# Weight tiles of two row blocks by 512 columns in the down and output projections, and up products in the order hi, hi, lo, lo

## Chip, cores and metric

The kernel runs on one core of a Trainium2 chip. The metric is the device time of one execution in microseconds (us), as the median of three runs. Beside it stands the trace of one profiled execution, whose span is counted from its first to its last instruction.

## What is computed

Two decoder layers on 256 tokens of width 2048, each an attention block and a squared-ReLU MLP, with a norm before and after each block. Cut to what matters here:

```python
D_MODEL, SEQ, D_FF = 2048, 256, 8192
def sq_relu_mlp(h, w_up, w_down):
    h = jax.nn.relu(h @ w_up)            # [256, 2048] @ [2048, 8192]
    return (h * h) @ w_down              # [256, 8192] @ [8192, 2048]

for l in range(2):
    h = rmsnorm(x, norm_attn_pre[l])
    mix = attention_l(h) @ w_o[l]        # output projection, [256, 2048] @ [2048, 2048]
    x = x + rmsnorm(mix, norm_attn_post[l])
    h = rmsnorm(x, norm_mlp_pre[l])
    x = x + rmsnorm(sq_relu_mlp(h, w_up[l], w_down[l]), norm_mlp_post[l])
```

Everything is float32. The weights amount to about 348 MB, each read once.

## The kernel before

[...] In the text below one "product" is one matmul instruction with its weight load. The 256 tokens are two halves of 128 (hf 0 and hf 1).

Weights come in tiles of 512 KB through `weights` (L115): SyncE issues the DMA into one of three `raw` buffers, ScalarE writes `hi`, VectorE writes `lo`, each into one of six buffers. TensorE takes them in the order of the program.

There are two ways of multiplying. With the activations stationary (`mm_tok`, L199, whose three products are L200, L201 and L202) the moving operand is 512 columns of weights, and a bank of PSUM holds [128 tokens, 512 columns]. `head_proj` (K and V, and the first 512 up features of an MLP) and `col_pass` (output projection and down projection) do so. With the weights stationary, `up_feat` (L496) makes the other up features: a bank per 128 features, where the hi part of a weight block meets x's hi and lo parts side by side (512 columns, L506), and the lo part meets x's hi part alone (256 columns, L507). `q_proj` (L268, L270, L271) does the same with three products of 256 columns.

`col_pass` (L390) covers 2048 rows by 1024 columns of a weight matrix with four banks, two column chunks c by two token halves. Its tile is one row block (128 rows) by 1024 columns; a tile serves 12 products, and the bank changes after every three. The last `ahead` tiles go to half 0 first; then half 0's two banks are taken away by `evac`, `between` follows, half 1 gets the same tiles, and its two banks are taken away. `head_proj` has tiles of two row blocks by 512 columns, and there six products in a row go to one bank:

```python
for j in range(2):
    k = 2 * i + j
    mm_tok(acc[hf], *halves(xT, k, hf), hl[0][:, j], hl[1][:, j], k == 0, k == KT - 1)
```

An output projection is two passes (`o_proj`, L420), both on the four banks of tag "a", with `ahead` 1 and 5; its `evac` is a square sum on ScalarE and a multiplication by the gain on VectorE (`ug`, L429). A down projection is four times two passes (`mlp`), on tag "b" and then "a", with `ahead` 1 but for the layer's last, which has 5; its `evac` adds to an accumulator on VectorE (`mlp`, L460). After a layer's last pass `add_normed` (L168) makes the new x, half by half, and its transposes (L184) begin the next projection, or the result is stored.

A tile scheduler sets the order of instructions on each engine from the order of the code and its own estimates.

Of the kernel before, what the change touches and what calls it, by code (L numbers as in the profile page):

```python
"""Two decoder layers (sliding-window attention with sinks, then MoBA attention on a shared K/V),
each followed by a squared-ReLU MLP, on one core.

Float32 products: TensorE multiplies 12-bit significands in one pass, so every operand is split
exactly into hi + lo (float32r, 12 bits each), and a product is hi*hi + hi*lo + lo*hi, accumulated in
float32; what is left out lies below float32's own rounding.

With SEQ == MOBA_BLOCK there is one MoBA block: no block lies fully in the past, so the top-k part
is masked for every token by the shapes alone, and the own block is causal attention.
"""  # L10
# [17 lines left out]
P = 128  # L28
T = 256
NH = 2  # L30
D = 2048
KT = D // P
# [7 lines left out]
EPS = 1e-6  # L40
# chunks by which token half 0 runs ahead where it does; buffers of raw and of split weights
# [3 lines left out]
# rounds of the running projection after which a group's attention steps go: scores, transposes, mixes  # L45
# [10 lines left out]
def trunk(ctx: ExitStack, tc: tile.TileContext, x, w_qkv_a, sinks_a, w_o_a, kv_norm, w_kv_shared,  # L56
# [8 lines left out]
    # one table set serves every activation used here  # L65
    nc.scalar.preload_act_table_set("natural_log_exp_and_others")

    # ---- residual stream, by token half
# [9 lines left out]
    # ---- constants  # L78
    ident = pool.tile([P, P], F32, name="ident")
    make_identity(nc, ident)  # L80
    # the array's clock rises with use: work on nothing until x is there
# [6 lines left out]
    # gains that act on the contraction axis, as columns [p, kt]  # L88
# [13 lines left out]
    # minus the distance between query and key, for the second query block against both key blocks;  # L102
    # the last 128 columns are also the first block's
# [11 lines left out]
    # ---- weights, split on the way in  # L115
    def weights(src, shape, gain=None):
        """src: DRAM view [128, a, b] with a * b = 1024 -> its hi and lo parts. With a gain (index, k-tile),
        row block i is scaled by the gain's k-tile + i first."""
        raw = pool.tile([P, *shape], F32, tag="raw", bufs=RBUFS, name="raw")
        hi = pool.tile([P, *shape], F32R, tag="hi", bufs=WBUFS, name="hi")  # L120
        lo = pool.tile([P, *shape], F32R, tag="lo", bufs=WBUFS, name="lo")
        nc.sync.dma_start(raw, src)
        if gain is None:
            nc.scalar.activation(hi, raw, AF.Copy)  # L124
            nc.vector.tensor_sub(lo, raw, hi.bitcast(F32))  # L125
        else:
            for i in range(shape[0]):
                c = gain[0] * KT + gain[1] + i
                g = gcol[:, c:c + 1]
                nc.scalar.activation(hi[:, i], raw[:, i], AF.Copy, scale=g)  # L130
                nc.vector.scalar_tensor_tensor(lo[:, i], raw[:, i], g, hi[:, i].bitcast(F32),  # L131
                                               op0=ALU.mult, op1=ALU.subtract)
        return hi, lo
# [4 lines left out]
    # ---- norms  # L138
    def rstd_of(parts):
        """1 / sqrt(sum(parts) / D + EPS), by exp(-ln / 2) and a Newton step."""  # L140
# [19 lines left out]
    def x_rstd(hf):  # L160
        a = parts_tile()
        # x's transposes are awaited, its scale is not yet
        with tc.issue_after(turned[0]):
            for c in range(4):
                square_sum(a[:, c:c + 1], xs[hf][:, c * 512:(c + 1) * 512])
        return rstd_of(a)

    def add_normed(hf, ug, parts, each):  # L168
        """x += rstd(parts) * ug, by columns of 512; each(c) follows."""
# [6 lines left out]
    def to_T(dst, name):  # L176
        """x's 512 columns c of a token half, transposed into dst: [d, kt, (hi: both halves | lo: both halves)]."""
# [20 lines left out]
    # ---- products with the activations stationary: out [tok, n]  # L198
# [5 lines left out]
    def head_proj(xT, w, c0, gi, second=None):  # L204
        """x @ 512 columns of w from c0, by token half; half 0 starts ahead. second() makes half 1's xT."""
# [22 lines left out]
    def kv_evac(acc, r):  # L228
        """k as [d; d] rows by group (hi | lo) and v as (hi | lo) columns by group."""
# [24 lines left out]
    # ---- products with the weights stationary: out [n, tok]  # L254
    def q_proj(xT, w, g, gi):
        """The eight heads of group g, [d, tok] / 8, as rows [hi; lo] (even heads) or [lo; hi] (odd); the
        tokens' rstd is left to the scores."""
        acc = [bank("a", f"q{i}") for i in range(2)]
        for i in range(KT // 2):
            hi, lo = weights(rows(w, 2 * i, 2, g * 512, 512), (2, 512), (gi, 2 * i))  # L260
            for j in range(2):
                k = 2 * i + j
                t = xT[k // 4][:, k % 4]
                for f in range(4):
                    o = acc[f // 2][:, (f % 2) * T:(f % 2 + 1) * T]
                    fs = slice(f * P, (f + 1) * P)
                    # the first product into the bank clears it; the bank's other half then starts from clear
# [19 lines left out]
    # ---- attention, in steps that run between the rounds of a projection  # L287
# [5 lines left out]
    def rounds(n):  # L293
        """n rounds of a projection have been issued: issue the steps that are due."""
# [7 lines left out]
    def attention(g, qs, ks, vs, oT, dist, with_sink, r, std):  # L302
        def scores(qb, hp):
# [6 lines left out]
            for e in range(2):  # L310
# [4 lines left out]
                # score = (q k + bias std) rstd  # L315
# [43 lines left out]
        def mix(qb, b):  # L359
# [6 lines left out]
            # rows 0-63 came of v's hi part, rows 64-127 of its lo part; odd heads go to the upper rows  # L366
# [23 lines left out]
    def col_pass(xT, w, r0, p, tag, ahead, evac, between=None):  # L390
        """x @ w[r0:r0 + 2048, p * 1024:...] by token half: the last `ahead` row blocks go to half 0 first.
        evac(hf, c, bank) takes the sums away; between() follows half 0's."""
        ps = [[bank(tag, f"o{hf}{c}") for c in range(2)] for hf in range(NH)]

        def step(hf, k, hl):
            for c in range(2):
                cs = slice(c * 512, (c + 1) * 512)
                mm_tok(ps[hf][c], *halves(xT, k, hf), hl[0][:, cs], hl[1][:, cs], k == 0, k == KT - 1)

        tail = []  # L400
        for k in range(KT):
            r = r0 + k * P
            hl = weights(w[r:r + P, p * 1024:(p + 1) * 1024], (1024,))
            step(0, k, hl)
            rounds(1)
            if k < KT - ahead:
                step(1, k, hl)
                rounds(1)
            else:
                tail.append((k, hl))  # L410
        for c in range(2):
            evac(0, 2 * p + c, ps[0][c])
        if between:
            between()
        for k, hl in tail:
            step(1, k, hl)
        for c in range(2):
            evac(1, 2 * p + c, ps[1][c])

    def o_proj(oT, w, gain, each):  # L420
        """x += rmsnorm(o @ w) * gain."""
# [9 lines left out]
        col_pass(oT, w, 0, 0, "a", 1, evac)  # L431
# [3 lines left out]
    # ---- MLP  # L435
    def mlp(xT, wu, wd, gi, gain, r_of, each):
        """x += rmsnorm(relu(rmsnorm(x) @ wu)^2 @ wd) * gain."""
# [33 lines left out]
    def over_partitions(r):  # L471
        """The two columns r, as rows side by side on every partition."""
# [9 lines left out]
    def up_tok(acc, r, hT):  # L482
        """relu(r acc)^2 of 512 features [tok, f], transposed."""
# [12 lines left out]
    def up_feat(xT, w, c0, gi, rb, hT, tag):  # L496
        """The same with the weights stationary: x's hi and lo parts side by side, summed on the way out."""
        acc = [bank(tag, f"u{f}") for f in range(4)]
        for i in range(KT // 2):
            hi, lo = weights(rows(w, 2 * i, 2, c0, 512), (2, 512), (gi, 2 * i))  # L500
            for f in range(4):
                fs = slice(f * P, (f + 1) * P)
                for j in range(2):
                    k = 2 * i + j
                    t = xT[k // 4][:, k % 4]
                    nc.tensor.matmul(acc[f], hi[:, j, fs], t, start=(k == 0), stop=False, skip_group_check=True)  # L506
                    nc.tensor.matmul(acc[f][:, :T], lo[:, j, fs], t[:, :T], start=False, stop=(k == KT - 1),  # L507
                                     skip_group_check=True)
        for f in range(4):
# [21 lines left out]
    # ---- two layers  # L531
# [54 lines left out]
```

## Time and profile before

| | |
|---|---|
| Median of three runs | 1967.25 us (1966.46 to 1967.7) |
| Profiled execution | span 1962.4 us; its own time is not given apart from the runs |
| Median less span | 4.85 us, start and end of the execution |
| TensorE busy | 1934.3 us, 99% of the span, 10318 products |
| TensorE weight loads busy | 1653.1 us, beside the products |
| VectorE / ScalarE / GpSimd busy | 1276.7 / 1096.5 / 245.4 us |
| DMA | 354.22 MB, mean 181 GB/s |
| Granted TensorE clock, mean | 0.998 of full speed |

Products overlap in their records: one of 512 columns is recorded as about 0.39 us long, and the next starts some 0.23 us after it. So the busy share doesn't tell how fast products follow each other. The distance from start to start does, and the timeline shows it. A name such as `o<-hi,h` is output, then moving and stationary operand.

### The profile page before, as it was taken

What the parts mean: (1) busy time and instruction counts of PE and PEld (TensorE: products, weight loads), DVE (VectorE), ACT (ScalarE), POOL (GpSimd) and SP (SyncE); (2) the same over time, 40 slices, a digit from 0 to 9 for tenths busy, and PEclk for the clock granted to TensorE, in tenths of its full rate; (3) what the DMA queues carried; (4) which work ended last, traced back from release to release, by engine and by line L of the source; (5) the groups of instructions that cost most, each with busy time, mean ns of one, the idle gap of its engine ahead of it and who ended that gap; (6) DMA issues with size and microseconds to landing.
All of it is one profiled execution on the core that took longest, in us unless ns stands there. A gap on an engine that the chain in (4) does not pass through costs nothing.

```text
span 1962.4 us, 28154 instructions
## 1 busy us (share of the span) xinstructions
PE 1934.3 (99%) x10318; PEld 1653.1 (84%) x10318; DVE 1276.7 (65%) x2177; ACT 1096.5 (56%) x1977; POOL 245.4 (13%) x306
## 2 busy tenths in 40 slices
PE   8999999999999999999999999999999999999997
PEld 7998788888888888888889988888888888888886
DVE  6898577546655664675588884875466457556654
ACT  7787565445544553554477874754455345435542
POOL 0242001000100110010112420010011001100111
PEclk9999999999999999999999999999999999999999
DMA  7534656666666666666554446566666666666663
GB/s 227 161 109 149 196 163 212 196 192 191 185 191 194 183 188 191 181 189 195 168 165 150 128 148 194 166 201 198 189 183 192 199 189 183 193 192 188 187 189 123
DMA packets 140682, 354.22 MB, mean 181 GB/s; under 512 B 10912, under 2 KB 11008, under 8 KB 140032
## 3 DMA queue, kind: packets, MB, share of 16 engines
q1 hardware_dynamic: 139776, 348.17, 58.4%
q10 hardware_dynamic: 736, 4.24, 0.6%
q8 instruction: 81, 1.33, 0.3%
q14 instruction: 57, 0.47, 0.1%
q0 software_dynamic: 32, 0.02, 0.0%
HBM read 350.28 MB, written 2.10 MB: 180 GB/s over the span
## 4 chain that ended last, share of the span: by engine, by line
PE 86%; DVE 5%; ACT 5%; DMA 2%; issue 1%; DVEq 0%; POOL 0%; ACTq 0%; SPq 0%
PE u L506 23%; PE o L202 14%; PE o L201 14%; PE o L200 14%; PE u L507 12%; ACT pr L338 1%; PE q L271 1%; PE q L268 1%; PE q L270 1%; ACT hi L130 1%; PE kv L200 1%; DVE pr L325 1%; PE kv L201 1%; PE kv L202 1%; DVE lo L131 1%
## 5 line engine op out<-in xcount | busy, mean ns | idle before, releaser
L506 PE MATMUL u<-xm,hi 128*128 128x512 f32 x1920 | 676.1, 397 | 0.0
L131 DVE SCALAR_TENSOR_TENSOR lo<-raw,gcol,hi 128x512 fp32r<-128x512 f32 x672 | 487.6, 756 | 192.8 <-ACT hi L130 181.8
L125 DVE TENSOR_TENSOR lo<-raw,hi 128x1024 fp32r<-128x1024 f32 x320 | 396.5, 1239 | 328.4 <-ACT hi L124 323.9
L130 ACT ACTIVATE hi<-raw,gcol 128x512 fp32r<-128x512 f32 x672 | 455.4, 716 | 257.6 <-PE u L506 114.8
L124 ACT ACTIVATE hi<-raw 128x1024 fp32r<-128x1024 f32 x320 | 338.6, 1059 | 404.4 <-PE o L202 320.4
L507 PE MATMUL u<-xm,lo 128*128 128x256 f32 x1920 | 539.3, 281 | 0.0
L506 PEld LDWEIGHTS u<-xm,hi 128*128 128x128 f32 x1920 | 360.4, 188 | 87.2
L202 PE MATMUL o<-hi,h 128*128 128x512 f32 x1024 | 401.7, 392 | 0.0
L201 PE MATMUL o<-lo,h 128*128 128x512 f32 x1024 | 401.4, 392 | 0.0
L200 PE MATMUL o<-hi,h 128*128 128x512 f32 x1024 | 399.1, 390 | 0.0
L507 PEld LDWEIGHTS u<-xm,lo 128*128 128x128 f32 x1920 | 362.9, 189 | 0.3
L514 POOL TENSOR_TENSOR us<-us,rb 128x256 f32<-128x256 f32 x120 | 115.8, 965 | 1268.1 <-DVE us L513 1268.1
L200 PEld LDWEIGHTS o<-hi,h 128*128 128x128 f32 x1024 | 192.3, 188 | 42.9
L201 PEld LDWEIGHTS o<-lo,h 128*128 128x128 f32 x1024 | 192.3, 188 | 42.7
L202 PEld LDWEIGHTS o<-hi,h 128*128 128x128 f32 x1024 | 192.4, 188 | 40.3
L268 PE MATMUL q<-xa,hi 128*128 128x256 f32 x512 | 147.1, 287 | 0.0
L271 PE MATMUL q<-xa,lo 128*128 128x256 f32 x512 | 144.8, 283 | 0.0
L270 PE MATMUL q<-xa,hi 128*128 128x256 f32 x512 | 144.4, 282 | 0.0
L516 ACT ACTIVATE h<-uh 128x256 fp32r<-128x256 f32 x120 | 50.2, 418 | 101.1 <-DVE uh L515 101.1
L200 PE MATMUL o<-hi,o 128*128 128x512 f32 x256 | 101.5, 398 | 2.1 <-DVE ug L429 2.0
L202 PE MATMUL o<-hi,o 128*128 128x512 f32 x256 | 101.1, 395 | 0.4 <-POOL o L378 0.4
L515 DVE SCALAR_TENSOR_TENSOR uh<-us 128x256 f32<-128x256 f32 x120 | 50.8, 423 | 77.5 <-POOL us L514 77.5
(116 smaller groups left out, 1902.6 us busy)
## 6 DMA issues: line engine op xcount, KB each, us to landing
raw<-in_w_up_dram SPq DMA_DIRECT2D x256, 512.0 KB, 4.2
raw<-in_w_down_dram SPq DMA_DIRECT2D x256, 512.0 KB, 4.5
raw<-in_w_qkv_a_dram SPq DMA_DIRECT2D x40, 512.0 KB, 4.4
raw<-in_w_o_a_dram SPq DMA_DIRECT2D x32, 512.0 KB, 4.5
raw<-in_w_q_b_dram SPq DMA_DIRECT2D x32, 512.0 KB, 3.9
raw<-in_w_o_b_dram SPq DMA_DIRECT2D x32, 512.0 KB, 3.8
raw<-in_w_kv_shared_dram SPq DMA_DIRECT2D x8, 512.0 KB, 4.0
x<-in_x_dram SPq DMA_DIRECT2D x8, 256.0 KB, 5.2
```

The lines of the kernel that those rows point to most:

```text
L124: nc.scalar.activation(hi, raw, AF.Copy)
L125: nc.vector.tensor_sub(lo, raw, hi.bitcast(F32))
L130: nc.scalar.activation(hi[:, i], raw[:, i], AF.Copy, scale=g)
L131: nc.vector.scalar_tensor_tensor(lo[:, i], raw[:, i], g, hi[:, i].bitcast(F32), op0=ALU.mult, op1=ALU.subtract)
L200: nc.tensor.matmul(ps, xh, wh, start=first, stop=False)
L201: nc.tensor.matmul(ps, xh, wl, start=False, stop=False)
L202: nc.tensor.matmul(ps, xl, wh, start=False, stop=last)
L268: nc.tensor.matmul(o, hi[:, j, fs], t[:, :T], start=(k == 0 and f % 2 == 0), stop=False, skip_group_check=True)
L270: nc.tensor.matmul(o, hi[:, j, fs], t[:, T:], start=False, stop=False, skip_group_check=True)
L271: nc.tensor.matmul(o, lo[:, j, fs], t[:, :T], start=False, stop=(k == KT - 1), skip_group_check=True)
L506: nc.tensor.matmul(acc[f], hi[:, j, fs], t, start=(k == 0), stop=False, skip_group_check=True)
L507: nc.tensor.matmul(acc[f][:, :T], lo[:, j, fs], t[:, :T], start=False, stop=(k == KT - 1), skip_group_check=True)
```

## The change

`col_pass` takes tiles of two row blocks by 512 columns instead of one by 1024, so six products in a row go to a bank. A tile of column chunk c is used by both halves, then the chunk changes; at the end of a pass the last row blocks of chunk 0 come before those of chunk 1 (`late`). `evac` follows a bank's last product at once. The first pass of the output projection has `ahead` 2 instead of 1. In `up_feat` the two row blocks' hi products of a feature chunk come first, then the two lo products.

```diff
     def col_pass(xT, w, r0, p, tag, ahead, evac, between=None):
         ps = [[bank(tag, f"o{hf}{c}") for c in range(2)] for hf in range(NH)]
-        def step(hf, k, hl):
-            for c in range(2):
-                cs = slice(c * 512, (c + 1) * 512)
-                mm_tok(ps[hf][c], *halves(xT, k, hf), hl[0][:, cs], hl[1][:, cs], k == 0, k == KT - 1)
+        n = KT // 2
+        def step(hf, i, c, hl):
+            for j in range(2):
+                k = 2 * i + j
+                mm_tok(ps[hf][c], *halves(xT, k, hf), hl[0][:, j], hl[1][:, j], k == 0, k == KT - 1)
+            if i == n - 1:
+                evac(hf, 2 * p + c, ps[hf][c])
+        late = (ahead + 1) // 2
+        tiles = [(i, c) for i in range(n - late) for c in range(2)]
+        tiles += [(i, c) for c in range(2) for i in range(n - late, n)]
         tail = []
-        for k in range(KT):
-            r = r0 + k * P
-            hl = weights(w[r:r + P, p * 1024:(p + 1) * 1024], (1024,))
-            step(0, k, hl)
+        for t, (i, c) in enumerate(tiles):
+            hl = weights(rows(w, r0 // P + 2 * i, 2, p * 1024 + c * 512, 512), (2, 512))
+            step(0, i, c, hl)
             rounds(1)
-            if k < KT - ahead:
-                step(1, k, hl)
+            if t < len(tiles) - ahead:
+                step(1, i, c, hl)
                 rounds(1)
             else:
-                tail.append((k, hl))
-        for c in range(2):
-            evac(0, 2 * p + c, ps[0][c])
+                tail.append((i, c, hl))
         if between:
             between()
-        for k, hl in tail:
-            step(1, k, hl)
-        for c in range(2):
-            evac(1, 2 * p + c, ps[1][c])
+        for i, c, hl in tail:
+            step(1, i, c, hl)
...
-        col_pass(oT, w, 0, 0, "a", 1, evac)
+        col_pass(oT, w, 0, 0, "a", 2, evac)
...
             for f in range(4):
                 fs = slice(f * P, (f + 1) * P)
                 for j in range(2):
                     k = 2 * i + j
-                    t = xT[k // 4][:, k % 4]
-                    nc.tensor.matmul(acc[f], hi[:, j, fs], t, start=(k == 0), stop=False, skip_group_check=True)
-                    nc.tensor.matmul(acc[f][:, :T], lo[:, j, fs], t[:, :T], start=False, stop=(k == KT - 1),
+                    nc.tensor.matmul(acc[f], hi[:, j, fs], xT[k // 4][:, k % 4], start=(k == 0), stop=False,
                                      skip_group_check=True)
+                for j in range(2):
+                    k = 2 * i + j
+                    nc.tensor.matmul(acc[f][:, :T], lo[:, j, fs], xT[k // 4][:, k % 4, :T], start=False,
+                                     stop=(k == KT - 1), skip_group_check=True)
```

The first place is TensorE at the start of the first down pass of layer 0, before the change. `o00` is the bank of half 0 and chunk 0, `o11` that of half 1 and chunk 1; the moving operand is a part of a weight tile, the stationary one a part of the MLP's hidden activations `h00`.

```order
L200 MATMUL o00_4090<-hi_4095,h00_3177 128x512
L201 MATMUL o00_4090<-lo_4096,h00_3177 128x512
L202 MATMUL o00_4090<-hi_4095,h00_3177 128x512
L200 MATMUL o01_4091<-hi_4095,h00_3177 128x512
L201 MATMUL o01_4091<-lo_4096,h00_3177 128x512
L202 MATMUL o01_4091<-hi_4095,h00_3177 128x512
L200 MATMUL o10_4092<-hi_4095,h00_3177 128x512
L201 MATMUL o10_4092<-lo_4096,h00_3177 128x512
L202 MATMUL o10_4092<-hi_4095,h00_3177 128x512
```

The bank changes after every three products. The same place on TensorE after the change:

```order
L200 MATMUL o00_4090<-hi_4095,h00_3177 128x512
L201 MATMUL o00_4090<-lo_4096,h00_3177 128x512
L202 MATMUL o00_4090<-hi_4095,h00_3177 128x512
L200 MATMUL o00_4090<-hi_4095,h00_3177 128x512
L201 MATMUL o00_4090<-lo_4096,h00_3177 128x512
L202 MATMUL o00_4090<-hi_4095,h00_3177 128x512
L200 MATMUL o10_4092<-hi_4095,h00_3177 128x512
L201 MATMUL o10_4092<-lo_4096,h00_3177 128x512
L202 MATMUL o10_4092<-hi_4095,h00_3177 128x512
```

Six products (two row blocks) now go to `o00` before the other half's bank `o10` follows with the same tile.

The second place is TensorE in `up_feat`, before the change; `u0` to `u3` are the banks of four feature chunks, `xm00` a part of x, `hi` and `lo` a weight tile.

```order
L506 MATMUL u0_4686<-xm00_3060,hi_4715 128x512
L507 MATMUL u0_4686<-xm00_3060,lo_4716 128x256
L506 MATMUL u0_4686<-xm00_3060,hi_4715 128x512
L507 MATMUL u0_4686<-xm00_3060,lo_4716 128x256
L506 MATMUL u1_4687<-xm00_3060,hi_4715 128x512
```

The 512-column and the 256-column products take turns. The same place on TensorE after the change (x2 is two such instructions in a row):

```order
L508 MATMUL u0_4686<-xm00_3060,hi_4715 128x512 x2
L512 MATMUL u0_4686<-xm00_3060,lo_4716 128x256 x2
L508 MATMUL u1_4687<-xm00_3060,hi_4715 128x512 x2
L512 MATMUL u1_4687<-xm00_3060,lo_4716 128x256 x2
L508 MATMUL u2_4688<-xm00_3060,hi_4715 128x512 x2
```

Two of 512 columns are followed by two of 256, still four products per bank.

The third place is VectorE where the two passes of layer 0's output projection meet, before the change; `lo_...<-raw` is a split of a weight tile, `ug` the multiplication that frees a bank.

```order
L125 TENSOR_TENSOR lo_2843<-raw_2841,hi_2842 128x1024
L125 TENSOR_TENSOR lo_2861<-raw_2859,hi_2860 128x1024
L429 TENSOR_TENSOR ug0_2186<-o00_2190,grow_2184 128x512
L429 TENSOR_TENSOR ug0_2186<-o01_2191,grow_2184 128x512
L429 TENSOR_TENSOR ug1_2187<-o10_2192,grow_2184 128x512
L429 TENSOR_TENSOR ug1_2187<-o11_2193,grow_2184 128x512
```

After the change, where the same multiplications are on L432:

```order
L125 TENSOR_TENSOR lo_2843<-raw_2841,hi_2842 128x1024
L432 TENSOR_TENSOR ug0_2186<-o00_2190,grow_2184 128x512
L432 TENSOR_TENSOR ug0_2186<-o01_2191,grow_2184 128x512
L432 TENSOR_TENSOR ug1_2187<-o10_2192,grow_2184 128x512
L125 TENSOR_TENSOR lo_2861<-raw_2859,hi_2860 128x1024
L432 TENSOR_TENSOR ug1_2187<-o11_2193,grow_2184 128x512
```

The multiplications stand one split earlier, and a split lies between the third and the fourth.

## Rows read from the trace of the kernel before

**Rows 1.** The page: span, and busy time of each engine (x instructions).

```profile
span 1962.4 us, 28154 instructions
PE 1934.3 (99%) x10318; PEld 1653.1 (84%) x10318; DVE 1276.7 (65%) x2177; ACT 1096.5 (56%) x1977; POOL 245.4 (13%) x306
```

**Rows 2.** The page: the chain that ended last, share of the span by engine.

```profile
PE 86%; DVE 5%; ACT 5%; DMA 2%; issue 1%; DVEq 0%; POOL 0%; ACTq 0%; SPq 0%
```

**Rows 3.** Groups of TensorE instructions by line: shape, count, busy us, mean ns, idle before.

```profile
L506 PE MATMUL u<-xm,hi 128*128 128x512 f32 x1920 | 676.1, 397 | 0.0
L507 PE MATMUL u<-xm,lo 128*128 128x256 f32 x1920 | 539.3, 281 | 0.0
L202 PE MATMUL o<-hi,h 128*128 128x512 f32 x1024 | 401.7, 392 | 0.0
...
L202 PE MATMUL o<-hi,o 128*128 128x512 f32 x256 | 101.1, 395 | 0.4 <-POOL o L378 0.4
```

**Rows 4.** Windows: length, busy PE, PEld, DVE, ACT, POOL (x), PEclk, DMA share, GB/s.

```profile
292.20:357.50 65.30, 65.30 (x380) 57.59 (x379) 45.50 (x73) 38.54 (x65) 8.41 (x8) 1.00 0.67 206
...
445.50:535.90 90.40, 90.40 (x513) 78.44 (x512) 58.64 (x96) 50.00 (x86) 12.65 (x12) 1.00 0.64 186
535.90:623.70 87.80, 87.80 (x386) 72.07 (x385) 46.51 (x53) 37.80 (x44) 2.96 (x4) 1.00 0.64 192
...
1264.00:1330.70 66.70, 66.70 (x381) 57.86 (x380) 46.32 (x75) 38.41 (x65) 7.99 (x8) 1.00 0.67 204
...
1418.60:1507.40 88.80, 88.80 (x513) 78.25 (x513) 57.98 (x95) 49.92 (x86) 12.62 (x12) 1.00 0.63 185
```

**Rows 5.** Timeline of TensorE, second down pair of layer 0: start, length.

```profile
535.93 0.39 PE L200 MATMUL o<-hi,h 128*128 128x512 f32 x1
...
623.82 0.40 PE L506 MATMUL u<-xm,hi 128*128 128x512 f32 x1
```

**Rows 6.** Timeline of TensorE, `head_proj` of layer 0.

```profile
28.02 0.39 PE L200 MATMUL kv<-hi,xa 128*128 128x512 f32 x1
...
34.82 0.39 PE L200 MATMUL kv<-hi,xa 128*128 128x512 f32 x1
```

**Rows 7.** Timeline of TensorE, a stretch of layer 0's output projection.

```profile
179.31 0.40 PE L200 MATMUL o<-hi,o 128*128 128x512 f32 x1
...
184.21 0.40 PE L200 MATMUL o<-hi,o 128*128 128x512 f32 x1
```

**Rows 8.** Timeline of TensorE, `q_proj` of layer 0.

```profile
43.24 0.28 PE L268 MATMUL q<-xa,hi 128*128 128x256 f32 x1
...
44.68 0.28 PE L268 MATMUL q<-xa,hi 128*128 128x256 f32 x1
```

**Rows 9.** What TensorE waited for: us in total, times, longest.

```profile
PE o L200 <- DVE ug L429: 2.0, 2, 1.6
...
PE pt L184 <- DVE x L173: 1.2, 2, 0.8
```

**Rows 10.** Timeline, between the passes of layer 0's output projection.

```profile
217.16 0.39 PE L202 MATMUL o<-hi,o 128*128 128x512 f32 x1
...
218.37 2.48 DVE L429 TENSOR_TENSOR ug<-o,grow 128x512 f32<-128x512 f32 x4
...
219.11 0.50 PE L200 MATMUL o<-hi,o 128*128 128x512 f32 x1 [1.57 <-DVE ug L429]
```

**Rows 11.** Timeline of the end: last product, last sums, their norm.

```profile
1951.77 0.40 PE L202 MATMUL o<-hi,h 128*128 128x512 f32 x1
1951.89 1.28 DVE L460 TENSOR_TENSOR mlp<-o,mlp 128x512 f32<-128x512 f32 x2
1953.98 0.16 DVE L142 TENSOR_REDUCE stat<-parts 128x1 f32<-128x4 f32 x1 [0.80 <-ACT junk L153]
```

**Rows 12.** DMA issues: count, KB each, us from issue to landing.

```profile
raw<-in_w_up_dram SPq DMA_DIRECT2D x256, 512.0 KB, 4.2
raw<-in_w_down_dram SPq DMA_DIRECT2D x256, 512.0 KB, 4.5
```

## Prediction

> **What bounds the kernel now.** First the page: TensorE is busy for 1934.3 us of a span of 1962.4 us, 99%, and no other engine for more than 65% of it [rows 1]. The chain that ended last says the same: 86% of it is TensorE, 5% each VectorE and ScalarE [rows 2]. So an edit counts if it changes how fast products follow each other on TensorE, or one of the few waits between them.
>
> The busy share can't tell the first, since products overlap: 512 columns are recorded as 392 to 397 ns [rows 3], while 384 of them fit into 87.89 us [rows 5]. So I read distances from start to start. The reader is to see four things.
>
> - A down pass pair makes 384 products of 512 columns from 535.93 to 623.82 us: 228.9 ns each, 686.7 ns for three [rows 5]. The other down pairs read alike.
> - `head_proj`, same shapes, goes through 30 products in 6.80 us, 226.7 ns each, 680.0 ns for three [rows 6]. All four runs of it settle there within a few products, and no stretch of `col_pass` does.
> - A stretch of the output projection takes 4.90 us for 21 products, 233.3 ns each, 700.0 for three [rows 7].
> - The up stretches between down pairs have two lengths for the same 512 products: 90.4 us and 88.8 us, that is 353.1 and 346.9 ns for a pair of 512 and 256 columns. The first stretch of layer 0 has the short pace too (65.3 us for its 377 products), that of layer 1 the long one (66.7 us). So 7 of the 30 calls of `up_feat` go fast and 23 slowly [rows 4].
>
> The granted clock is 1.00 in all of these windows [rows 4], the level of 2.4 GHz. There 512 columns last 213.3 ns, so a product costs 13.4, 15.6 or 20.0 ns beyond its columns, and this remainder differs between places with equal shapes. In none of these stretches does TensorE wait.
>
> **The change part by part.**
>
> *Six products per bank.* The down and output projections have 1024 + 256 groups of three products [rows 3]; their number, shapes and weight loads stay. What changes is that a bank gets six products of two row blocks, from a tile of two row blocks by 512 columns. That is what `head_proj` does, in its part where the token halves take turns, and rows 6 are from this part. No row shows it inside `col_pass`, so I bound it: at best 680.0 ns for three, the pace of [rows 6], 6.7 ns less than now, 1280 × 6.7 = 8.5 us gained; at worst 700.0 ns [rows 7], 13.3 ns more, 17.1 us lost. I take the first, since the order of banks, moving tiles and stationary parts is then that of `head_proj`. What stays different is where the stationary operand lies: activations of the MLP or of attention, not x. That is what I am unsure of.
>
> *Hi, hi, lo, lo.* The 1920 pairs now cost 448 × 346.9 + 1472 × 353.1 ns = 675.2 us. The new order makes 960 groups of four: two of 512 columns, two of 256. Products of 256 columns in a row stand in `q_proj`: 12 in 1.44 us, 120.0 ns each [rows 8], so a weight load is covered by 256 columns there. For the two of 512 columns I have 226.7 to 233.3 ns [rows 6, 7]. The group costs 693.4 ns at best, 706.6 ns at worst. I take 228.9 ns, the pace of the longest run of them [rows 5]: 2 × 228.9 + 2 × 120.0 = 697.8 ns, 669.9 us in all, a gain of 5.3 us. The ends are a gain of 9.5 and a loss of 3.1 us.
>
> *The meeting of the two passes of the output projection.* Both use the same four banks. Now all four sums of half 0 and half 1 come free in a bunch: the last product of the first pass starts at 217.16 us, VectorE begins the four multiplications at 218.37, and TensorE starts the second pass at 219.11 [rows 10]. In both layers together this wait is 2.0 us [rows 9]. With the change a bank is taken away as soon as its last product is through, and from there to the first product of the new pass in the same bank 18 others follow (4.1 us), for each of the four. The split put between the third and fourth multiplication (1.2 us on VectorE) fits into that. I take the whole 2.0 us; the bounds are 0 and 2.0.
>
> *The end.* After the last product VectorE adds two chunks in 1.28 us before the norm starts [rows 11]. Chunk 0's sum of half 1 will be ready three tiles earlier and be taken away beside products, so half of it goes, 0.6 us; the norm and the store behind it stay.
>
> *The layer's ends in between.* Half 0's chunk 0 is likewise taken away three tiles earlier, so its norm starts up to 0.6 us sooner; TensorE now waits 1.2 us for x there, in two places [rows 9]. But VectorE works through splits of coming weights between the steps of that norm, which decide as much. I take 0.7 us, within 0 and 1.2.
>
> *The transfers.* Same bytes and count per tile, in runs of 2 KB instead of 4 KB. The up tiles have such runs already: they land 4.2 us after issue, the down tiles 4.5 us [rows 12], and a down tile lasts 12 × 228.9 ns = 2.7 us with three in flight. The DMA share is 0.63 to 0.65 in either kind of stretch [rows 4]. I count nothing. What hides it is that lead: ScalarE is busy 37.8 us of a pair's 87.8 [rows 4], so it catches up after a late tile. Without this cover each late tile would stop TensorE by what it is late.
>
> *Sum.* 8.5 + 5.3 + 2.0 + 0.6 + 0.7 = 17.1 us. From the profiled execution: 1962.4 − 17.1 = 1945.3 us of span, and 4.85 us around it, the distance of that span to the median of the runs, makes 1950 us.
>
> **The rivals.**
>
> *Neither pace moves.* The remainder per product is something that the order of products doesn't touch; then only the waits go, 3.3 us, 1964 us. For it: the two paces of `up_feat` come out of one and the same order, and so don't follow from the order alone [rows 4]. Against it: `head_proj` and `col_pass` have equal shapes and keep apart every time [rows 5, 6]. [...]
>
> *One pace moves, the other doesn't.* The projections reach 680.0 ns and the up products stay: 8.5 + 3.3 us, 1955 us. Or the up products gain and the projections stay at 686.7: 5.3 + 3.3, 1959 us. For it: the two edits share no product.
>
> *The projections fall into the slow pace.* The place is `col_pass` in all down passes: 700.0 ns for three, as in [rows 7], where the same code runs at that pace for 21 products without a wait. With the other terms kept that is 17.1 − 5.3 − 3.3 = 8.5 us more, 1976 us. It decides from 696.5 ns for three on: there the loss, 9.8 × 1280 = 12.5 us, has eaten the other 8.6 us and 3.9 us (0.2%) besides. Against it: it occurs only in the output projections, among attention's products.
>
> **How the numbers follow.** Both paces move as in the sum: 0.45, 1950 us. One of them: 0.22, 1955 to 1959 us. Neither: 0.15, 1964 us. Slow pace: 0.15, 1976 us. The remaining 0.03 is for what I don't see. The range reaches from 1943 us (the sum with 9.5 for the up products and 1.2 for the layers' ends is 1945; 2 us for finer errors) to 1970 us (neither pace, with the up products' 3.1 us loss, is 1967; the same margin and a little). It leaves out the slow pace and the rest. 0.2% is 3.9 us, about what a measurement of this kernel can tell from no change. Faster by more: both, one, and a small part of neither, 0.71. Within it: most of neither, 0.13. Slower: 0.16.
>
> **What would show it.** In the changed kernel's timeline: three products of a down pass in 680 ns, a down pair of 384 in 87.0 us instead of 87.9; four up products in about 698 ns, a stretch of 512 in 89.3 us, alike in all layers; no wait of L200 for `ug`; a norm that begins 0.6 us sooner after the last product. The prediction is wrong if the down pairs still take 87.9 us or 89.6 us (700 ns for three), if products of 512 columns in a row are slower in `up_feat` than anywhere before, or if TensorE begins to wait for `hi` or `lo` in the down passes.

## The result, and the profile after

In all that follows, every operand stands as the sum of two parts, hi and lo, and the product of two operands is made as three matmuls: hi hi, hi lo and lo hi.

| | before | after |
|---|---|---|
| Median | 1966.86 us (4 runs, 1966.29 to 1967.7) | 1956.03 us (4 runs, 1955.51 to 1957.04) |
| Ratio | | 0.9945, 95% interval 0.9933 to 0.9957 |
| Span of the profiled execution | 1962.4 us | 1954.3 us |

The time fell by 10.8 us, 0.55%. Span and median differ by 4.5 us before and by 1.7 us after, so the two spans alone make the gain look smaller, 8.1 us. The table before the change calls its 4.85 us the start and end of the execution, and that is wrong: in every run whose span is on record the time exceeds the span by 1.7 to 2.1 us. The rest is that the profiled execution of before was a short one. One reason shows: from 14 to 18 us its granted clock was 1.00, the level of 2.4 GHz, where the profile after has a mean of 0.81 and a second profile of before (run 11 below, span 1965.0 us) one of 0.55, so that both spent part of that time at 1.2 GHz. The forecast is not touched by this, since it adds the same 4.85 us back.

The page of the changed kernel, span and busy time, beside [rows 1]:

```profile
span 1954.3 us, 28151 instructions
PE 1928.2 (99%) x10318; PEld 1649.4 (84%) x10318; DVE 1273.6 (65%) x2177; ACT 1097.2 (56%) x1977; POOL 247.1 (13%) x306
```

TensorE is the bound as before, with the same number of products. Its windows, two up stretches of layer 0, a down pair, and two up stretches of layer 1 (columns as in [rows 4]):

```profile
291.35:357.16 65.81, 65.81 (x381) 57.46 (x380) 46.43 (x75) 38.61 (x66) 8.41 (x8) 1.00 0.71 210
445.07:534.25 89.18, 89.18 (x513) 77.81 (x512) 58.58 (x97) 49.84 (x86) 12.66 (x12) 1.00 0.65 188
534.25:622.16 87.91, 87.91 (x386) 72.13 (x385) 47.90 (x55) 37.78 (x44) 2.95 (x4) 1.00 0.64 190
1259.50:1325.30 65.80, 65.80 (x381) 57.45 (x379) 46.47 (x75) 38.80 (x67) 8.14 (x8) 1.00 0.68 206
1413.20:1502.40 89.20, 89.20 (x514) 77.83 (x513) 58.59 (x97) 49.81 (x86) 12.53 (x12) 1.00 0.65 189
```

The reader is to see two things. An up stretch of 512 products takes 89.2 us in either layer, where [rows 4] had 90.4 and 88.8: 696.7 ns for two pairs. The down pair takes 87.91 us for its 384 products, as in [rows 5]: 228.9 ns each, 687 for three. Six products per bank changed nothing there.

What TensorE waits for, the longest waits, beside [rows 9]:

```profile
PE po L364 <- ACT ph L355: 2.4, 4, 1.0
PE kv L200 <- ACT xa L187: 2.1, 1, 2.1
PE po L365 <- DVE pl L356: 1.7, 5, 0.6
PE pt L184 <- DVE x L173: 1.7, 2, 1.5
```

The wait for `ug` is gone from the whole list. The waits of the transposes (L184) for x have grown, from 1.2 to 1.7 us, the longest from 0.8 to 1.5. Another wait of the kernel before, in the K and V projection of layer 1, is gone instead:

```profile
PE kv L201 <- DVE stat L145: 0.7, 1, 0.7
```

The place of the wait for `ug` in the timeline after the change, beside [rows 10]:

```profile
217.63 1.89 DVE L432 TENSOR_TENSOR ug<-o,grow 128x512 f32<-128x512 f32 x3
...
218.08 0.39 PE L202 MATMUL o<-hi,o 128*128 128x512 f32 x1
...
218.37 0.50 PE L200 MATMUL o<-hi,o 128*128 128x512 f32 x1
```

The second pass starts 0.29 us after the last product of the first, where there were 1.95 us. At the end of the kernel, beside [rows 11], VectorE has one chunk left to add:

```profile
1944.23 0.40 PE L202 MATMUL o<-hi,h 128*128 128x512 f32 x1
1944.67 0.69 DVE L463 TENSOR_TENSOR mlp<-o,mlp 128x512 f32<-128x512 f32 x1 [0.19 <-PE o L202]
1946.15 0.16 DVE L142 TENSOR_REDUCE stat<-parts 128x1 f32<-128x4 f32 x1 [0.79 <-ACT junk L153]
```

Where the gain came from, in us, by stretches from one stage's first product to the next's in the two timelines:

| stretch | before | after | difference |
|---|---|---|---|
| eight up stretches | 678.1 | 671.5 | -6.5 |
| output projections (two) | 209.8 | 207.9 | -1.9 |
| K and V projection of layer 1, and the down pair ahead of it | 117.6 | 116.6 | -1.0 |
| last down pair to the end | 98.3 | 97.7 | -0.6 |
| the other six down pairs | 527.4 | 527.4 | 0.0 |

These make -10.0 us. The rest, +1.9 us in this pair of traces, lies in the start and in the attention stretches, which the change doesn't touch and which differ by as much between the two profiles of the kernel before: 1.4 us in the K and V projection of layer 0 and 1.1 us in the attention stretch of layer 1.

### The profile page after: what moved, and what is told of

It is laid out like the page before. It is cut to its first block, busy times and chain, and to the rows that moved or that the text cites. A ratio compares the mean times of both kernels' runs of the same rounds, so it can differ in the third digit from the quotient of the medians.

```text
span 1954.3 us, 28151 instructions
## 1 busy us (share of the span) xinstructions
PE 1928.2 (99%) x10318; PEld 1649.4 (84%) x10318; DVE 1273.6 (65%) x2177; ACT 1097.2 (56%) x1977; POOL 247.1 (13%) x306
## 4 chain that ended last, share of the span: by engine, by line
PE 87%; DVE 5%; ACT 5%; DMA 2%; issue 1%; POOL 0%; DVEq 0%; ACTq 0%; SPq 0%
PE u L508 23%; PE o L200 15%; PE o L202 15%; PE o L201 14%; PE u L512 11%; ACT pr L338 1%; DVE lo L131 1%; DVE pr L325 1%; ACT hi L130 1%; PE kv L200 1%; PE kv L201 1%; PE kv L202 1%; PE q L271 1%; PE q L268 1%; PE q L270 1%
## 5 line engine op out<-in xcount | busy, mean ns | idle before, releaser
L508 PE MATMUL u<-xm,hi 128*128 128x512 f32 x1920 | 603.5, 395 | 0.0
L512 PE MATMUL u<-xm,lo 128*128 128x256 f32 x1920 | 377.9, 278 | 0.0
L508 PEld LDWEIGHTS u<-xm,hi 128*128 128x128 f32 x1920 | 293.0, 189 | 0.7
```

The source lines that it names most:

```text
L508: nc.tensor.matmul(acc[f], hi[:, j, fs], xT[k // 4][:, k % 4], start=(k == 0), stop=False, skip_group_check=True)
L512: nc.tensor.matmul(acc[f][:, :T], lo[:, j, fs], xT[k // 4][:, k % 4, :T], start=False, stop=(k == KT - 1), skip_group_check=True)
```

## Experiments

The open question was why the down and output projections kept their 687 ns for three products. **Theory S**, later made precise as **theory R**: the pace is set by where the stationary operand lies in memory beside the moving one. In the built programs each tile has a fixed byte offset within a partition; weights and x begin at 96 modulo 128, the projections' stationary operands (attention output, hidden activations) at 32, and the change alters none of these. **Rival H**: a stretch takes over its pace from what ran before it and keeps it. Two more runs share the gain out among the parts of the change.

**1. The up order alone.** The kernel before, with this part of the change:

```diff
                 for j in range(2):
                     k = 2 * i + j
-                    t = xT[k // 4][:, k % 4]
-                    nc.tensor.matmul(acc[f], hi[:, j, fs], t, start=(k == 0), stop=False, skip_group_check=True)
-                    nc.tensor.matmul(acc[f][:, :T], lo[:, j, fs], t[:, :T], start=False, stop=(k == KT - 1),
+                    nc.tensor.matmul(acc[f], hi[:, j, fs], xT[k // 4][:, k % 4], start=(k == 0), stop=False,
                                      skip_group_check=True)
+                for j in range(2):
+                    k = 2 * i + j
+                    nc.tensor.matmul(acc[f][:, :T], lo[:, j, fs], xT[k // 4][:, k % 4, :T], start=False,
+                                     stop=(k == KT - 1), skip_group_check=True)
```

> The kernel before with the up order hi, hi, lo, lo alone. Theory A (the up order is what pays, through the pace of up_feat): the up stretches of 512 products take 89.2 us each, in every layer, as in the changed kernel, instead of 90.4 or 88.8; the time falls by 6 to 8 us, to about 1959.5. Rival B (the waits at the ends of passes carry the gain, and the up stretches' paces differ from execution to execution anyway): under 2 us, 1965 or more.

Measured: 1960.13 us (5 runs, 1959.98 to 1962.21) beside 1966.69 us of before on the same chip, ratio 0.9968 (0.9956 to 0.9981), 6.6 us less. One up stretch and the down pair after it:

```profile
445.70:534.86 89.16, 89.16 (x513) 77.80 (x512) 58.48 (x96) 49.95 (x87) 12.67 (x12) 1.00 0.64 189
534.86:622.77 87.91, 87.91 (x386) 72.12 (x385) 46.60 (x53) 37.77 (x44) 2.96 (x4) 1.00 0.64 193
```

All six full up stretches take 89.2 us. Theory A holds: the order pays by the pace.

**2. The projections' part alone.** The changed kernel with the old up order:

```diff
                 for j in range(2):
                     k = 2 * i + j
-                    nc.tensor.matmul(acc[f], hi[:, j, fs], xT[k // 4][:, k % 4], start=(k == 0), stop=False,
+                    t = xT[k // 4][:, k % 4]
+                    nc.tensor.matmul(acc[f], hi[:, j, fs], t, start=(k == 0), stop=False, skip_group_check=True)
+                    nc.tensor.matmul(acc[f][:, :T], lo[:, j, fs], t[:, :T], start=False, stop=(k == KT - 1),
                                      skip_group_check=True)
-                for j in range(2):
-                    k = 2 * i + j
-                    nc.tensor.matmul(acc[f][:, :T], lo[:, j, fs], xT[k // 4][:, k % 4, :T], start=False,
-                                     stop=(k == KT - 1), skip_group_check=True)
```

> The changed kernel with the old up order, so the new tiles, the earlier sums and ahead 2 alone. Theory A: only waits go, 2.0 us where the output projection's passes meet and 0.6 us at the end; 1964 us, down stretches of 384 products still 87.9 us, up stretches at 90.4 or 88.8. Rival B: most of the gain is here, 1958 to 1960.

Measured: 1962.22 us (11 runs, 1961.41 to 1965.54), ratio 0.9979 (0.997 to 0.9988), 4.5 us less. Down pairs take 87.9 us, up stretches 88.8 or 90.4:

```profile
447.20:535.95 88.75, 88.75 (x514) 78.25 (x513) 58.53 (x97) 49.72 (x85) 12.63 (x12) 1.00 0.65 187
535.95:623.84 87.89, 87.89 (x386) 72.11 (x385) 47.92 (x56) 37.78 (x44) 2.97 (x4) 1.00 0.64 193
623.84:714.28 90.44, 90.44 (x513) 78.39 (x512) 59.51 (x98) 49.32 (x84) 12.62 (x12) 1.00 0.64 188
```

So no pace moved, and what went is waits: 4.5 us where theory A said 2.6. A left out the K and V projection of layer 1, which is 0.8 us shorter in this trace. The two parts, 6.6 and 4.5, make 11.1 us beside the 10.8 measured for both together, well within the intervals.

**3. The changed kernel with 64 unused bytes** per partition, so that the projections' stationary operands begin at 96 modulo 128, like the weights:

```diff
+        pad = pool.tile([P, 16], F32, tag="pad", bufs=1, name="pad")
+        nc.gpsimd.memset(pad, 0.0)
         ks = pool.tile([P, HKV, 2, T], F32R, tag="k", bufs=1, name="ks")
```

> The changed kernel with 64 bytes per partition of unused memory put ahead of the tiles of k, so that the stationary operands of the projections begin at the same place modulo 128 bytes as weights and x do (they are 64 bytes off in both kernels). Theory S (the projections' pace is set by where the stationary operand lies beside the moving one, not by the order): three products go from 687 to 680 ns as in head_proj, 1280 x 6.7 = 8.6 us less, 1947.5. Rival H (the pace is taken over from what ran before, up_feat, and kept): no change, 1956, 687 ns.

Measured: 1948.01 us (4 runs, 1947.9 to 1949.73), ratio 0.9907 (0.9892 to 0.9922). An up stretch and the down pair behind it:

```profile
444.87:534.03 89.16, 89.16 (x513) 77.80 (x512) 58.61 (x97) 49.84 (x86) 12.66 (x12) 1.00 0.65 189
534.03:621.08 87.05, 87.05 (x386) 72.07 (x385) 47.83 (x55) 37.80 (x44) 2.97 (x4) 1.00 0.65 191
```

The down pair goes from 87.91 to 87.05 us, 680 ns for three, with every instruction in the same order as in the changed kernel but for the fill of the unused bytes. What runs ahead of it is the same up stretch. H falls, S holds, in its size too: 8.0 us of the 8.6 expected.

**4. The kernel before with the same 64 bytes.** The same two lines, put into the kernel before.

> The kernel before with the same 64 bytes. Theory S alone: three products per bank reach 680 ns too, 8.6 us less, 1958. If place and six products per bank are both needed: 687 ns, 1967, while the changed kernel with the 64 bytes reaches 680. Rival H: 687 ns in both, 1967.

Measured: 1962.06 us (11 runs, 1957.78 to 1965.34), ratio 0.9974 (0.9965 to 0.9983), 4.6 us less. The windows:

```profile
449.50:539.94 90.44, 90.44 (x513) 78.47 (x512) 58.61 (x96) 50.00 (x86) 12.60 (x12) 1.00 0.64 186
539.94:627.01 87.07, 87.07 (x387) 72.08 (x385) 46.58 (x53) 37.77 (x44) 2.98 (x4) 1.00 0.64 195
```

With three products per bank the down pairs reach 680 ns for three as well. The place alone does it: at both places tried with both orders of banks, the order has no part in the pace. The time gave back only half of the 8.6 us. In this profile seven of the eight up stretches have the long pace (before: six), 1.7 us, and the output projection of layer 0 takes 2.0 us longer. Most of the latter is clock. TensorE waited 1.9 us for `ug` where the two passes meet, and then the granted clock fell, to a mean of 0.75 and 0.83 in two windows of 4 us:

```profile
221.00:225.00 4.00, 3.54 (x11) 2.87 (x12) 3.32 (x5) 1.67 (x5) 0.00 (x0) 0.75 0.69 232
225.00:229.00 4.00, 4.00 (x16) 3.18 (x15) 1.22 (x1) 1.20 (x2) 0.00 (x0) 0.83 0.51 137
```

In between, eight products follow each other at 0.43 us instead of 0.23, the level of 1.2 GHz, which costs 1.6 us. Whether that is so in the other ten runs no profile tells; two of them, 1957.78 and 1958.38 us, are where theory S put the time.

**5. Everything at 0 modulo 128.** Run 3's lines, and unused bytes ahead of x's tiles:

```diff
+    pad0 = pool.tile([P, 8], F32, name="pad0")
+    nc.gpsimd.memset(pad0, 0.0)
     xT = []
     turn_x = to_T(xT, "xa0")
```

> The changed kernel with 32 unused bytes per partition ahead of x's transposed tiles and 64 ahead of k, so that all operands of products begin at a multiple of 128 bytes. Theory R (what counts is the place of the stationary operand relative to the moving one, modulo 128): as with the 64 bytes alone, 680 ns for three products, 1948. Theory L (the remaining 13 ns per product come from beginning off a multiple of 64, so full alignment takes more away): three products under 675 ns, the up stretches under 88 us, 1930 or less.

Measured: 1948.35 us (4 runs, 1945.98 to 1949.58), ratio 0.9894 (0.9877 to 0.991). Down pair 87.06 us, up stretch 89.17 us, as in run 3. L falls: starting at a multiple of 128 bytes takes nothing off the 680 ns.

**6. x at 32.** Three pads: ahead of x's tiles, behind them, and run 3's ahead of k:

```diff
+    pad0 = pool.tile([P, 16], F32, name="pad0")
+    nc.gpsimd.memset(pad0, 0.0)
     xT = []
     turn_x = to_T(xT, "xa0")
     for c in range(4):
         turn_x(0, c)
+    pad1 = pool.tile([P, 16], F32, name="pad1")
+    nc.gpsimd.memset(pad1, 0.0)
```

> The changed kernel with x's transposed tiles at 32 modulo 128, weights and the projections' stationary operands at 96. Theory R (relative place): head_proj, whose stationary operand is x, goes from 680 to 687 ns for three; the projections at 680; up_feat and q_proj, where x is the moving operand, change their pace too. Theory P (the stationary operand's own place, 32 being slow): head_proj 687, projections 680, up_feat and q_proj as in the changed kernel. Rival H (pace taken over from what ran before): head_proj stays at 680.

Measured, one run: 1946.12 us. `head_proj` goes at 687 ns for three, the projections at 680, and up stretches take 88.76 us: all three kinds moved. (Run 12 has the lines of the same kernel.) The projections and `head_proj` have changed roles against the changed kernel, with the same code. Against run 3 only x's tiles have moved modulo 128, and only the products that read x have changed their pace. R holds, P has its first two marks but not the third.

**7. The projections' stationary operand at 0, weights at 96**, by a longer pad ahead of k alone:

```diff
+        pad = pool.tile([P, 24], F32, tag="pad", bufs=1, name="pad")
+        nc.gpsimd.memset(pad, 0.0)
         ks = pool.tile([P, HKV, 2, T], F32R, tag="k", bufs=1, name="ks")
```

> The changed kernel with the projections' stationary operands at 0 modulo 128, weights at 96, a distance of 32 bytes where the changed kernel has 64. Theory R: neither 680 nor necessarily 687 ns for three; if the distance modulo 64 counts, up to 700. Theory P: 680, if only 32 is a bad place.

Measured, one run: 1973.62 us, 17.6 more than the changed kernel's median, but on a chip where the kernel before took 2.4 us more than in the result. In the traces the down pairs are 13.4 us longer than the changed kernel's and the output projections 1.6, 15.0 together. The down pair:

```profile
539.18:628.78 89.60, 89.60 (x387) 72.15 (x385) 47.96 (x55) 37.80 (x44) 2.96 (x4) 1.00 0.62 187
```

700 ns for three, the pace of [rows 7] and of the third rival of the prediction, now from start to end of every down pass. P falls.

**8. Everything at 32.** As run 5, with a longer pad ahead of x's tiles:

```diff
-    pad0 = pool.tile([P, 8], F32, name="pad0")
+    pad0 = pool.tile([P, 16], F32, name="pad0")
```

> The changed kernel with all operands of products at 32 modulo 128. Theory R: distance 0 everywhere, so 680 ns for three in head_proj and in the projections, about 1948. Theory P: 687 ns in both, about 1957.

Measured, one run: 1948.57 us; down pair 87.07 us, up stretch 89.16 us. R: distance 0, wherever the operands lie.

**9. x and the projections' stationary operands at 64.** As run 6, with other pads:

```diff
-    pad0 = pool.tile([P, 16], F32, name="pad0")
+    pad0 = pool.tile([P, 24], F32, name="pad0")
...
-    pad1 = pool.tile([P, 16], F32, name="pad1")
+    pad1 = pool.tile([P, 8], F32, name="pad1")
...
-        pad = pool.tile([P, 16], F32, tag="pad", bufs=1, name="pad")
+        pad = pool.tile([P, 8], F32, tag="pad", bufs=1, name="pad")
```

> The changed kernel with x's transposed tiles and the projections' stationary operands at 64 modulo 128, weights at 96. Stationary less moving is then 96 in head_proj and in the projections, 32 in up_feat and q_proj, two distances not seen there yet. Theory R, if the pace depends on the distance alone: head_proj and the projections agree with each other, whatever it is; 700 ns for three if 96 is as 32 (a symmetric rule), 680 or less if the order counts. Rival: head_proj and the projections differ, so something else in them counts too.

Measured, one run: 1979.61 us. An up stretch and a down pair, then two products of `head_proj` that lie ten groups of three apart:

```profile
451.23:541.17 89.94, 89.94 (x513) 78.41 (x512) 58.66 (x97) 49.90 (x86) 12.62 (x12) 1.00 0.64 185
541.17:630.77 89.60, 89.60 (x386) 71.98 (x385) 47.97 (x55) 37.77 (x44) 2.96 (x4) 1.00 0.64 189
```

```profile
27.77 0.39 PE L200 MATMUL kv<-hi,xa 128*128 128x512 f32 x1
...
34.77 0.39 PE L200 MATMUL kv<-hi,xa 128*128 128x512 f32 x1
```

700 ns for three in both, so they agree, and 96 is as 32.

**10. x at 0.** As run 6, with other pads:

```diff
-    pad0 = pool.tile([P, 16], F32, name="pad0")
+    pad0 = pool.tile([P, 8], F32, name="pad0")
...
-    pad1 = pool.tile([P, 16], F32, name="pad1")
+    pad1 = pool.tile([P, 24], F32, name="pad1")
```

> The changed kernel with x's transposed tiles at 0, weights and the projections' stationary operands at 96. Stationary less moving is 32 in head_proj, 0 in the projections, 96 in up_feat and q_proj. Theory R: head_proj 700 ns for three as the projections were at 32, projections 680; up_feat at some new pace, alike in all eight stretches.

Measured, one run: 1955.43 us. `head_proj` at 700 ns for three (7.00 us for ten groups), projections at 680, the six full up stretches at 90.02 us and the two shorter ones at 68.61, alike in both layers. As R says.

**11. The kernel before, profiled again**, with no edit.

> The kernel before, unchanged, profiled once more. If the two paces of up_feat (88.8 and 90.4 us for 512 products) are picked anew in each execution: other stretches go fast than in the first profile. If they are fixed by the program: stretch 1 of layer 0 and stretch 2 of layer 1 are fast again, the others slow.

Measured: 1967.13 us, span 1965.0. The first up stretch of layer 0 in the first profile, then the same one and the next two in this one:

```profile
289.67:357.60 67.93, 67.92 (x396) 59.63 (x395) 48.13 (x79) 40.29 (x68) 8.41 (x8) 1.00 0.68 207
```

```profile
291.01:360.18 69.17, 69.16 (x395) 59.80 (x394) 49.06 (x80) 40.35 (x68) 8.43 (x8) 1.00 0.71 210
448.10:536.85 88.75, 88.75 (x514) 78.25 (x513) 58.44 (x96) 49.86 (x86) 12.64 (x12) 1.00 0.65 188
624.74:715.18 90.44, 90.44 (x514) 78.47 (x512) 60.49 (x100) 49.34 (x84) 12.65 (x12) 1.00 0.65 187
```

From product to product, the first stretch took 67.9 us in the first profile and takes 69.2 us now, and the second fell from 90.4 to 88.75. So the same program has other stretches at the short pace in another execution. The program has some part in it all the same: in the four profiles with the old order (before twice, runs 2 and 4) a short-paced stretch is always the first or second of its layer, never the third or fourth. What picks the pace stays open.

**12. The kernel of run 6, timed.**

> The kernel with x's transposed tiles at 32 and everything else of the products at 96 modulo 128 again, timed. By the stretches seen so far: projections 680 ns for three (distance 0), 8 x 0.4 us less in the up stretches than at distance 0, some 0.4 us lost in head_proj: about 1945.5 us, below the 1948.0 of the changed kernel with 64 bytes and the 1956.0 of the changed kernel. Rival (the one look at it was a favourable execution): 1948 or more.

Measured: 1942.98 us (4 runs, 1940.95 to 1946.15), ratio 0.9878 (0.9862 to 0.9895). An up stretch and a down pair, then two products of `head_proj`, ten groups of three apart (687 ns each):

```profile
445.21:533.97 88.76, 88.76 (x513) 77.87 (x512) 58.55 (x97) 49.80 (x86) 12.66 (x12) 1.00 0.65 190
533.97:621.03 87.06, 87.06 (x387) 72.10 (x385) 47.83 (x55) 37.80 (x44) 2.95 (x4) 1.00 0.65 191
```

```profile
27.54 0.39 PE L200 MATMUL kv<-hi,xa 128*128 128x512 f32 x1
...
34.41 0.39 PE L200 MATMUL kv<-hi,xa 128*128 128x512 f32 x1
```

The shortest of all medians: 13 us below the changed kernel, with the same instructions in the same order but for the fills of the unused bytes. It is 2.5 us below what the stretches let expect, and the profiled run, at 1946.15 us, was the longest of the four; the other three were not profiled.

## Why the prediction held, and where it didn't

The direction held and the size only in part: 1950 us forecast, 1956.0 measured, inside the range. It came out as the second rival, one pace moves and the other doesn't, 1959 us for the up products. The range held because it was drawn to take in this case, not because the sum was right: its largest term, half of the 17.1 us, came to nothing.

- *Six products per bank* (forecast: 8.5 us): nothing. This is the step that failed, the pace at which the projections' products follow each other. I read the difference between `head_proj` and `col_pass` as one of order, and named the other one, where the stationary operand lies, as the thing I was unsure of. Runs 3 and 4 show that it is this other one: 64 bytes give 680 ns for three with either order. The 8.5 us are real (8.0 in run 3), but the change doesn't reach them.
- *Hi, hi, lo, lo* (forecast 5.3 us): 6.6 us in run 1, 6.5 in the stretches. I had 697.8 ns for the group of four; it is 696.7. How it is composed came out otherwise: two products of 512 columns are 233 and 233 ns apart and those of 256 some 115, where I had 228.9 and 120.0. The two errors cancel, so the group's size came out by luck. The old order's share of long stretches varies from execution to execution (run 11), which I took as fixed.
- *Meeting of the passes* (2.0 us): the wait is gone, and the two output projections are 1.9 us shorter, as forecast and for the reason forecast.
- *The end* (0.6): 0.6 us. Of these, 0.3 lie ahead of the norm (it begins 2.2 us after the last product before, 1.9 now), half of what I expected there, and the rest within it.
- *The layers' ends* (0.7): 1.0 us, of which 0.8 are in the K and V projection of layer 1 and 0.2 in the down pair ahead of it; the second profile of before has those 0.2 too, so they are not the change's. The size is near by luck. I expected TensorE to wait less for x, and it waits 0.5 us longer; what went is its wait of 0.7 us for `stat`, in the middle of that K and V projection, which I had not looked at.
- *The transfers* at nothing: right. TensorE's waits name no weight tile, and the DMA share in the down pair stays at 0.64.
- *First rival, neither pace moves*, falls: the up products did gain. The projections alone kept theirs, and run 3 and run 7 give 226.7 and 233.3 ns to the same products in the same order. The Trainium skill, page "TensorE: Matmul & The Clock Gate", section "Back-to-back issue gap", gives about 216 ns for an isolated product of 512 columns and about 131 ns per product for a stream of weight loads and products. The traces agree with neither for these products, each with a weight load: they show more than one value for equal columns, and all of them above both.
- *Third rival, the slow pace*: it exists in all down passes in run 7, at a distance of 32, where the down pairs and output projections took 15.0 us more (I had 17.1). The stretch of [rows 7] that I took it from lies at a distance of 64, where some stretches have this pace and others don't (below).

## What to carry to other kernels

When equal instructions go at different paces at two places, list everything that differs between the places, operand addresses among it, before giving the difference to the one thing that the change touches. An operand's place costs a line to shift, so try it before reordering work: here 64 unused bytes per partition gave 8.0 us in the changed kernel, more than either part of the change, and 4.6 us in the kernel before. A stretch that has two paces in one program is a warning that its mean belongs to an execution; compare such stretches over several profiles.

## What the runs showed of the hardware

The pace of products of float32r operands with a weight load each depends on the distance between the stationary and the moving operand, modulo 128 bytes. These are the figures at a granted clock of 1.00, from the timelines; the group of four is that of the changed `up_feat`, and the distance is stationary less moving. In all these products one of the two operands is a weight tile, and ScalarE and VectorE meanwhile write other weight tiles at the same place modulo 128; no run separates the distance between the two operands from the distance to these writes.

| distance | three of 512 columns | group of four (2 x 512, 2 x 256) |
|---|---|---|
| 0 | 680 ns | 697 ns |
| 32 | 700 ns | 703 ns |
| 64 | 687 ns, in some stretches 700 ns | 693 ns |
| 96 | 700 ns | 703 ns |

So the best place differs with the shapes: 0 for products of 512 columns alone, 64 for the mixed group.

At distance 64, products of 512 columns have two paces. All down pairs of the five profiles with this distance (before twice, after, runs 1 and 2) go at 687 ns for three. But the second pass of layer 1's output projection goes at one pace in the first profile of before and at the other in the second, run 11. Here are its second and its last product, 190 products apart, in the first profile:

```profile
1191.36 0.39 PE L201 MATMUL o<-lo,o 128*128 128x512 f32 x1
...
1234.86 0.40 PE L202 MATMUL o<-hi,o 128*128 128x512 f32 x1
```

In the second profile:

```profile
1193.25 0.40 PE L201 MATMUL o<-lo,o 128*128 128x512 f32 x1
...
1237.59 0.40 PE L202 MATMUL o<-hi,o 128*128 128x512 f32 x1
```

That is 228.9 and 233.4 ns each, at a granted clock of 1.00, with one and the same program. The 700 ns of [rows 7] are of this kind: the same place goes at 680 ns with the 64 bytes (runs 3 and 4), and no such stretch at a distance of 0 went at 700 ns in any profile. What picks the pace at 64 stays open; rival H, which falls as the reason for 680 and 687 ns, isn't excluded for this choice.

For products of 256 columns alone, in `q_proj`, distance 64 is better too. [rows 8] has 120.0 ns each at 0, and in run 12, at 64, 24 products take 2.72 us, 113 ns each (in run 6, the same program, 118 ns in layer 1):

```profile
49.98 0.28 PE L272 MATMUL q<-xa,hi 128*128 128x256 f32 x1
...
52.70 0.28 PE L272 MATMUL q<-xa,hi 128*128 128x256 f32 x1
```

Only steps of 32 bytes were tried, and how the distance acts inside the chip stays open: the runs show that it does, not by what.
